# The heads' output-gate and bonus products of a hybrid decoder block formed from float32r parts with exact remainders

## The chip, the cores and the metric

The kernel runs on one core of one Trainium2 chip. The metric is the device time of one execution in microseconds (us), median of the runs. The five queues of the core are called by their engines: PE (TensorE: matrix products, with PEld for its weight loads), DVE (VectorE), ACT (ScalarE), POOL (GpSimd) and SP (SyncE, which issues nearly all DMA transfers). Each engine works its own queue in order and waits on semaphores for the others.

## The reference, cut to what matters

One decoder block over 256 tokens, width 2048, everything in float32: an RWKV-7 branch of 16 heads of 64 and a sliding-window attention branch of 16 heads work beside each other, are gated, added and projected, and a squared-ReLU MLP of width 8192 follows. The change touches two products of the RWKV branch, the gate `g` (160 gate inputs by 1024 columns) and the bonus (a sum over each head's 64 channels):

```python
p = h @ w_in[l] + b_in[l]                     # r, k, v, wd, ad, gd are columns of it
g = jax.nn.sigmoid(gd) @ g2                   # gd: 256 x 160, g2: 160 x 1024
...
y = rwkv7_scan(r_h, hs(decay), k_h, v_h, -kk, kk * a_h)
yn = ((y - mu) * lax.rsqrt(var + RWKV_GN_EPS)).reshape(B, T, C)
yn = yn * ln_w.astype(jnp.float32) + ln_b.astype(jnp.float32)
bonus = jnp.sum(r_h * k_h * r_k.astype(jnp.float32), axis=-1, keepdims=True) * v_h
out = (yn + bonus.reshape(B, T, C)) * g.astype(jnp.float32)
```

## The kernel before, in words

Activations lie transposed: channels on the 128 partitions, 256 tokens along the free axis. **The weight products** make up most of the time. Their weights come in blocks of 512 KB (tile `raw`, DMA of L286 on SP; the adaLN matrix in tiles `ada`, L141, which take their buffers from the same ring of 7). `split` (L264) halves each block into two float32r parts: ACT casts it to `whi` (L274), and DVE subtracts to get the exact remainder `wlo` (L275). `feed` (L297) and `rows_product` (L319) then form hi·hi, hi·lo and lo·hi products on PE, one float32r instruction each. Products of plain float32 tiles, with no such parts, remain in the heads' own work; there each product is two records in the trace.

**The RWKV heads** go through in four pieces (ss = 0 to 3) of four heads, two blocks of 128 channels each; every piece computes, per block i: the decay and key terms, `km` (r·k·r_k, one buffer), the products of `ar` with `bn` and `ke` (L566), which are masked into `tt` and stored to DRAM (`scr`, L573), the bonus product of `km` with the block-diagonal ones `bones` (L576), whose result is multiplied by v (L577), and transposes by identity products (`turned64`, L478). Two pieces at a time share one inversion of 16x16 blocks (`inverse16`): a load of `scr` into a tile of tag `lg` (L611), 30 small operations on POOL, two stores (L622, L624) and eight loads (L629), all on SP's queue. The products of the levels (L644, L653, L683) use what those loads bring. The output (`output`) normalises y, scales it on ACT (L745), loads the block's columns of g2 into a tile `lg` of two buffers (L748 for 128 of its rows, L749 for 32), transposes y (L478) and forms the gate product against `sgd` (L754, 128 rows) and `sgd2` (L755, 32 rows) in the same PSUM tile; ACT's L757, DVE's L759 and L760 finish the block.

**Order.** The code is written as three queues of generator steps (adaLN, attention, RWKV) which `pulse` advances by fixed rates while the weight blocks go by; from that, and from the buffers, a scheduler with a cost estimate of its own makes one fixed list of instructions for each engine and for SP. A tile of a tag with one buffer can't be written until the last reader of the one before is done.

## Time and profile before

| | |
|---|---|
| median of 3 runs | 1566.24 us (1565.78 to 1566.56) |
| the profiled execution | 1566.93 us, of which its span is 1565.1 us |
| PE busy | 1510.9 us, 97% of the span |
| DVE busy | 1100.7 us, 70% |
| ACT busy | 722.6 us, 46% |
| mean granted PE clock | 0.987 of full speed |
| moved by DMA | 372.80 MB, 238 GB/s in the mean |

The heads' work lies between about 190 and 700 us, the MLP behind 780 us. A start time in the rows below is us from the beginning of the span. A timeline row groups like neighbours: its second number lasts from the first one's start to the last one's end, and since products overlap in their pipeline, what a group costs is read from its start to the start of the next group.

### The profile page before, as it was taken

What the parts mean: (1) busy time and instruction counts of PE and PEld (TensorE: products, weight loads), DVE (VectorE), ACT (ScalarE), POOL (GpSimd) and SP (SyncE); (2) the same over time, 40 slices, a digit from 0 to 9 for tenths busy, and PEclk for the clock granted to TensorE, in tenths of its full rate; (3) what the DMA queues carried; (4) which work ended last, traced back from release to release, by engine and by line L of the source; (5) the groups of instructions that cost most, each with busy time, mean ns of one, the idle gap of its engine ahead of it and who ended that gap; (6) DMA issues with size and microseconds to landing.
All of it is one profiled execution on the core that took longest, in us unless ns stands there. A gap on an engine that the chain in (4) does not pass through costs nothing.

```text
span 1565.1 us, 30120 instructions
## 1 busy us (share of the span) xinstructions
PE 1510.9 (97%) x12122; PEld 1385.8 (89%) x12122; DVE 1100.7 (70%) x1784; ACT 722.6 (46%) x1107; POOL 40.5 (3%) x97
## 2 busy tenths in 40 slices
...
GB/s 343 335 325 295 342 234 245 245 170 310 283 262 285 269 155 297 282 147 339 285 215 173 240 222 228 216 222 226 225 228 211 227 222 205 184 188 189 194 183 81
DMA packets 297100, 372.80 MB, mean 238 GB/s; under 512 B 40912, under 2 KB 198384, under 8 KB 296320
## 3 DMA queue, kind: packets, MB, share of 16 engines
...
q0 software_dynamic: 512, 0.15, 0.1%
q14 instruction: 45, 0.37, 0.1%
...
## 4 chain that ended last, share of the span: by engine, by line
PE 87%; DVE 4%; DMA 3%; ACT 2%; issue 2%; POOL 1%; SPq 0%; POOLq 0%; DVEq 0%; ACTq 0%
PE mm L297 41%; PE mm L319 14%; PE ax L319 14%; PE ax L297 9%; PE ax L683 2%; PE ax L186 1%; PE ax L478 1%; DVE wlo L275 1%; DVE acc L219 1%; PE ax L566 1%; DMA ada<-in_w_ada_dram 1%; ACT whi L274 1%; DMA tt<-in_x_dram 1%; PE ax L653 0%; PE ax L237 0%
## 5 line engine op out<-in xcount | busy, mean ns | idle before, releaser
L274 ACT CAST whi<-raw 128x1024 fp32r<-128x1024 f32 x458 | 478.0, 1047 | 673.4 <-PE mm L297 257.0
L275 DVE TENSOR_TENSOR wlo<-raw,whi 128x1024 fp32r<-128x1024 f32 x458 | 557.0, 1219 | 267.3 <-ACT whi L274 258.6
L297 PE MATMUL mm<-h,whi 128*128 128x256 f32 (+1 forms) x3296 | 446.8, 286 | 3.4 <-ACT whi L274 3.4
L297 PEld LDWEIGHTS mm<-h,whi 128*128 128x128 f32 (+1 forms) x3296 | 415.2, 192 | 10.1 <-ACT whi L274 3.4
L219 DVE SCALAR_TENSOR_TENSOR acc<-ada,cact,acc 128x512 f32<-128x512 f32 x330 | 247.0, 749 | 60.2 <-DMA ada<-in_w_ada_dram 55.6
L297 PE MATMUL mm<-h,wlo 128*128 128x256 f32 (+1 forms) x1648 | 237.7, 284 | 0.0
L297 PEld LDWEIGHTS mm<-h,wlo 128*128 128x128 f32 (+1 forms) x1648 | 215.0, 191 | 1.1 <-issue 0.7
L319 PE MATMUL mm<-whi,u 128*128 128x512 f32 x512 | 138.3, 392 | 0.0
L319 PE MATMUL ax<-whi,u 128*128 128x512 f32 x512 | 138.0, 391 | 0.0
L297 PE MATMUL ax<-h,whi 128*128 128x256 f32 x768 | 109.0, 290 | 9.0 <-DVE p L969 4.5
L319 PEld LDWEIGHTS ax<-whi,u 128*128 128x128 f32 x512 | 96.2, 188 | 21.0
L319 PEld LDWEIGHTS mm<-whi,u 128*128 128x128 f32 x512 | 95.6, 188 | 20.2
L297 PEld LDWEIGHTS ax<-h,whi 128*128 128x128 f32 x768 | 100.2, 197 | 11.4 <-ACT whi L274 5.0
L319 PE MATMUL ax<-wlo,u 128*128 128x512 f32 x256 | 79.4, 391 | 0.0
L319 PE MATMUL mm<-wlo,u 128*128 128x512 f32 x256 | 79.3, 391 | 0.0
L297 PE MATMUL ax<-h,wlo 128*128 128x256 f32 x384 | 59.2, 287 | 0.0
L319 PEld LDWEIGHTS mm<-wlo,u 128*128 128x128 f32 x256 | 48.1, 188 | 10.5
L319 PEld LDWEIGHTS ax<-wlo,u 128*128 128x128 f32 x256 | 48.1, 188 | 10.5
L297 PEld LDWEIGHTS ax<-h,wlo 128*128 128x128 f32 x384 | 52.6, 197 | 0.1
L297 PE MATMUL mm<-tt,whi 128*128 128x256 f32 x256 | 37.7, 298 | 2.1 <-ACT tt L768 2.1
L297 PEld LDWEIGHTS mm<-tt,whi 128*128 128x128 f32 x256 | 34.5, 203 | 3.2 <-ACT tt L768 2.3
L319 PE MATMUL mm<-whi,m 128*128 128x512 f32 x128 | 35.0, 392 | 0.0
...
## 6 DMA issues: line engine op xcount, KB each, us to landing
ada<-in_w_ada_dram SPq DMA_DIRECT2D x192, 512.0 KB, 5.5
raw<-in_w_up_dram SPq DMA_DIRECT2D x128, 512.0 KB, 3.9
raw<-in_w_down_dram SPq DMA_DIRECT2D x128, 512.0 KB, 4.0
raw<-in_w_in_dram SPq DMA_DIRECT2D x72, 512.0 KB, 5.2
raw<-in_w_in_dram SPq DMA_DIRECT2D x128, 256.0 KB, 5.1
raw<-in_w_out_dram SPq DMA_DIRECT2D x32, 512.0 KB, 6.1
raw<-in_w_branch_attn_dram SPq DMA_DIRECT2D x16, 512.0 KB, 5.9
raw<-in_w_branch_rwkv_dram SPq DMA_DIRECT2D x16, 512.0 KB, 5.2
```

The costliest lines, as they stand in the source:

```text
L186: TE.matmul(ps[:, j:j + 1], lhsT=acc[:, j * P:(j + 1) * P], rhs=ones[:, 0:1], start=True, stop=True)
L219: V.scalar_tensor_tensor(o, in0=t[:, a, :], scalar=ck, in1=o, op0=ALU.mult, op1=ALU.add)
L274: S.copy(hi[:], raw[:])
L275: V.tensor_tensor(lo[:], raw[:], hi[:].bitcast(F32), op=ALU.subtract)
L297: TE.matmul(ps[0:m, j * tw:(j + 1) * tw], lhsT=wt[:, kk, o:o + m], rhs=xx(k), start=(k == begin and xx is xh and wt is hi and j == 0), sto ...
L319: TE.matmul(pss[tb][:], lhsT=uu(k)[:, sl], rhs=wt[:, kk, :], start=(first and k == 0), stop=(final and k == kblocks - 1))
L478: TE.matmul(out[hs, :], lhsT=src[hs, chunk(c)], rhs=ident[hs, hs], start=True, stop=True)
L566: TE.matmul(pT[hs, o:o + P], lhsT=src[hs, chunk(c)], rhs=ar[hs, i, c].rearrange("p a b -> p (a b)"), start=True, stop=True)
L683: TE.matmul(ps[hs, j, i, part, :], lhsT=lhs(j, i, hs), rhs=rhs(j, i, hs), start=(first and j == 0 and i == 0), stop=True, skip_group_check ...
```

## The change

Both kinds of product are formed from float32r parts, the way the weight products are. A helper `parts(hi, lo, x_)` casts on ACT and subtracts on DVE.

- **Bonus:** `km` is split into two tiles of tag `yn` (two buffers), and `bones` is cast once to `bonr`. One float32 product becomes two float32r ones (L584 and L585 in the changed kernel). `km` is free when DVE's subtraction has read it, no longer when PE has.
- **Gate:** `sgd` and `sgd2` are split once into `sgh`, `sgl` and the pair `sg2`; each block's g2 columns are split into `lh` and `ll` (one buffer each) from `lg`, which now has one buffer instead of two. Two float32 products a block become three of 128 rows (L767) and three of 32 rows (L769). `inverse16` takes the same single `lg` buffer.

```diff
--- before.py
+++ after.py
@@ -441,9 +441,10 @@
     tw = mx.tile([P, T], F32, name="tw")
-    sgd = mx.tile([P, T], F32, name="sgd")
-    kd = mx.tile([P, 2, T], F32, name="kd")
-    sgd2 = kd[0:32, 0, :]
+    sgh, sgl = [mx.tile([P, T], F32R, name=n) for n in ("sgh", "sgl")]
+    bonr = mx.tile([P, P], F32R, name="bonr")
+    kd = tl("kd", (2, T))
+    sg2 = []
     HS = [slice(0, L), slice(L, 2 * L)]
     state = [mx.tile([P, 2, 2, L], F32, name=nm("state")) for _ in range(2)]
@@ -471,6 +472,11 @@
+
+    def parts(hi, lo, x_):
+
+        S.copy(hi, x_)
+        V.tensor_tensor(lo, x_, hi.bitcast(F32), op=ALU.subtract)
     def turned64(out, src, c):
@@ -573,7 +579,10 @@
                 nc.sync.dma_start(square(scr[u:u + 4]).rearrange("u s t -> s u t"), tt[HS[p], 4 * i:4 * i + 4, 0, 0:L])
             yield
             pbn = ps_ax()
-            TE.matmul(pbn[:, 0:T], lhsT=bones, rhs=km[:], start=True, stop=True)
+            kmh, kml = [tl("yn", (T,), 2, F32R) for _ in range(2)]
+            parts(kmh[:], kml[:], km[:])
+            TE.matmul(pbn[:, 0:T], lhsT=bonr[:], rhs=kmh[:], start=True, stop=False)
+            TE.matmul(pbn[:, 0:T], lhsT=bonr[:], rhs=kml[:], start=False, stop=True)
             V.tensor_tensor(bv[:, i, :], vT, pbn[:, 0:T], op=ALU.mult)
             for n, (src, dst) in enumerate(((bn[:], "bt"), (ke, "kt"), (vT, "vt"))):
                 if n == 1:
@@ -607,7 +616,7 @@
     def inverse16(dds):
-        a16 = tl("lg", (16, 16), 2)
+        a16 = tl("lg", (16, 16))
         nc.sync.dma_start(a16[:], blocks16(scr[:]))
         x16 = tl("p4", (2, 16, 16), 2)
         tmp = tl("rs", (L,), 2)
@@ -743,16 +752,21 @@
             for c in range(NCH):
                 yc = y[:, i, chunk(c)]
                 S.activation(yc, yc, AF.Identity, bias=rd[:, 4 + c:5 + c], scale=rd[:, c:c + 1])
-            lg = tl("lg", (2, P), 2)
+            lg = tl("lg", (2, P))
             cl = slice(b * P, (b + 1) * P)
             nc.sync.dma_start(lg[:, 0, :], rwkv_g2[0:P, cl])
             nc.sync.dma_start(lg[0:32, 1, :], rwkv_g2[P:P + 32, cl])
             yield
+            lh, ll = [tl(n, (2, P), 1, F32R) for n in ("lh", "ll")]
+            for ks in ((slice(0, P), 0), (slice(0, 32), 1)):
+                parts(lh[ks], ll[ks], lg[ks])
             pF = ps_ax()
             for c in range(NCH):
                 turned64(pF[:, c * L:(c + 1) * L], y[:, i, :], c)
-            TE.matmul(pF[:, T:], lhsT=lg[:, 0, :], rhs=sgd[:], start=True, stop=False)
-            TE.matmul(pF[:, T:], lhsT=lg[0:32, 1, :], rhs=sgd2, start=False, stop=True)
+            for q, (w_, x_) in enumerate(((lh, sgh), (lh, sgl), (ll, sgh))):
+                TE.matmul(pF[:, T:], lhsT=w_[:, 0, :], rhs=x_[:], start=(q == 0), stop=False)
+            for q, (w_, x_) in enumerate(((lh, sg2[0]), (lh, sg2[1]), (ll, sg2[0]))):
+                TE.matmul(pF[:, T:], lhsT=w_[0:32, 1, :], rhs=x_, start=False, stop=(q == 2))
             yo = tl("yn", (T,), 2)
             S.activation(yo[:], pF[:, 0:T], AF.Identity, bias=colB[:, B_LB + b:B_LB + b + 1],
                          scale=colB[:, B_LW + b:B_LW + b + 1])
@@ -878,9 +892,12 @@
     def begin_heads():
         shifted(tw, e_l[:, 0:T], P, 24)
         S.activation(tw[0:L, :], tw[0:L, :], AF.Tanh)
+        sgd = tl("yn", (T,), 2)
         shifted(sgd, e_l[:, T:2 * T], P, 25)
         S.activation(sgd[:], sgd[:], AF.Tanh, scale=0.5)
         V.tensor_scalar(sgd[:], sgd[:], 1.0, 0.5, op0=ALU.add, op1=ALU.mult)
+        parts(sgh[:], sgl[:], sgd[:])
+        S.copy(bonr[:], bones)
         in0, in1 = [tl("in", (3, 2, T), 2) for _ in range(2)]
         for n, ((_, a_b), e) in enumerate(zip(A_RKV, (e_k, e_r, e_v))):
             for i in range(2):
@@ -995,9 +1012,13 @@
     def gd2():
         ps = cols_product(w_in, KC, O_WD + 256, [32], hA, hB)
+        sgd2 = tl("yn", (T,), 2)[0:32, :]
         shifted(sgd2, ps[0:32, 0:T], 32, 26)
         S.activation(sgd2, sgd2, AF.Tanh, scale=0.5)
         V.tensor_scalar(sgd2, sgd2, 1.0, 0.5, op0=ALU.add, op1=ALU.mult)
+        t = tl("kd", (2, T), 1, F32R)
+        sg2.extend(t[0:32, i, :] for i in range(2))
+        parts(*sg2, sgd2)
     def keyed(ss):
         for n in range(3):
```

Counted over PE's whole list, 24 float32 products of 128x256 go and 64 float32r products come; the stretches of float32r products between float32 ones number 123 before and 137 after.

Three places in the lists of instructions. First PE, at the first two heads' bonus products of the first two pieces (270 to 282 us before); L566 is L572 in the changed kernel, L478 is L484. Before:

```order
L297 MATMUL mm_2967<-h_219,wlo_3082 128x256 x8
L576 MATMUL ax_3113<-km_2934,kt 128x256
L478 MATMUL ax_3125<-kt,p_358_2633 64x64 x8
L297 MATMUL mm_2967<-h_219,whi_3177 128x256
L297 MATMUL mm_2967<-h_221,whi_3177 128x256
L478 MATMUL ax_3113<-kt,cs_2938 64x64 x8
L478 MATMUL ax_3125<-kt,in_2490 64x64 x8
```

and before, the second block's products, a little further on:

```order
L566 MATMUL ax_3022<-ar_2645,p_367_2650 64x128 x2
L566 MATMUL ax_3022<-ar_2645,cs_2952 64x128 x2
L566 MATMUL ax_3022<-ar_2645,p_367_2650 64x128 x2
L566 MATMUL ax_3032<-ar_2645,p_367_2650 64x128 x2
L566 MATMUL ax_3032<-ar_2645,cs_2952 64x128 x2
L566 MATMUL ax_3032<-ar_2645,p_367_2650 64x128 x2
L576 MATMUL ax_3144<-km_2948,kt 128x256
L478 MATMUL ax_3156<-kt,p_367_2650 64x64 x8
```

After:

```order
L297 MATMUL mm_2973<-h_219,wlo_3088 128x256 x2
L572 MATMUL ax_3028<-ar_2651,p_369_2656 64x128 x2
L572 MATMUL ax_3028<-ar_2651,cs_2958 64x128 x2
L572 MATMUL ax_3028<-ar_2651,p_369_2656 64x128 x2
L572 MATMUL ax_3038<-ar_2651,p_369_2656 64x128 x2
L572 MATMUL ax_3038<-ar_2651,cs_2958 64x128 x2
L572 MATMUL ax_3038<-ar_2651,p_369_2656 64x128 x2
L297 MATMUL mm_2973<-h_219,wlo_3088 128x256 x6
L584 MATMUL ax_3119<-yn_3120,bonr 128x256
L585 MATMUL ax_3119<-yn_3121,bonr 128x256
L484 MATMUL ax_3136<-kt,p_360_2639 64x64 x8
L584 MATMUL ax_3155<-yn_3156,bonr 128x256
```

What moved: the second block's six L572 rows now stand ahead of both bonus products, and its L584 stands close behind the first block's.

Second, SP around the first inversion (317 to 347 us before), with the semaphores each waits for; L611, L622, L624 and L748 are L620, L631, L633 and L757 in the changed kernel. The numbers in the names count tiles: raw_4150, 4191, 4249 and 4319 before are raw_4176, 4217, 4275 and 4345 after; ada_4187, 4279 and 4349 are ada_4213, 4305 and 4375. Before:

```order
L573 DMA scr<-tt_3021 64x4x64 [waits DMAHW1_49]
L286 DMA raw_4191<-in_w_in_dram 128x4x256 [waits DMAHW2_49,DVE_49]
L939 DMA grd<-gr_3814 128x512 [waits DMAHW3_49,Activation_49]
L611 DMA lg_3955<-scr 128x16x16 [waits DMAHW4_49,DMAHW1_49,DMAHW0_49]
L286 DMA raw_4249<-in_w_in_dram 128x4x256 [waits DMAHW5_49,DVE_49]
L141 DMA ada_4279<-in_w_ada_dram 128x2x512 [waits DMAHW6_49,DVE_49]
L748 DMA lg_5492<-in_rwkv_g_dram 128x128 [waits DMAHW7_49]
L286 DMA raw_4319<-in_w_in_dram 128x4x256 [waits DVE_49]
L141 DMA ada_4349<-in_w_ada_dram 128x2x512 [waits DVE_49]
L622 DMA scr_245<-p_536_3957 128x16x16 [waits DMAHW2_49,Pool_49]
```

After:

```order
L286 DMA raw_4176<-in_w_in_dram 128x4x256 [waits DMAHW0_49,DVE_49]
L620 DMA lg_3981<-scr 128x16x16 [waits DMAHW5_49,DMAHW6_49,DMAHW2_49,DMAHW1_49]
L141 DMA ada_4213<-in_w_ada_dram 128x2x512 [waits DVE_49]
L956 DMA grd<-gr_3840 128x512 [waits DMAHW3_49,Activation_49]
L286 DMA raw_4217<-in_w_in_dram 128x4x256 [waits DMAHW4_49,DVE_49]
L286 DMA raw_4275<-in_w_in_dram 128x4x256 [waits DVE_49]
L757 DMA lg_5522<-in_rwkv_g_dram 128x128 [waits DMAHW1_49,Pool_49]
L631 DMA scr_247<-p_546_3983 128x16x16 [waits DMAHW7_49,Pool_49]
L633 DMA scr_247<-p_546_3983 128x16x16 [waits DMAHW0_49,Pool_49]
L141 DMA ada_4305<-in_w_ada_dram 128x2x512 [waits DVE_49]
```

What moved: the g2 load (L757) waits for POOL; raw_4345 and ada_4375 left the place ahead of the two stores, and ada_4305 now stands behind them. On DVE the same weight blocks, before:

```order
L843 TENSOR_TENSOR m_3805<-m_3805 128x4
L844 RECIPROCAL m_3805<-m_3805 128x4
L219 SCALAR_TENSOR_TENSOR acc_4186<-ada_4349,cact,acc_4186 128x512
L275 TENSOR_TENSOR wlo_4119<-raw_4116,whi_4118 128x1024
L219 SCALAR_TENSOR_TENSOR acc_4186<-ada_4349,cact,acc_4186 128x512
L275 TENSOR_TENSOR wlo_4153<-raw_4150,whi_4152 128x1024
```

After:

```order
L857 TENSOR_TENSOR m_3831<-m_3831 128x4
L858 RECIPROCAL m_3831<-m_3831 128x4
L275 TENSOR_TENSOR wlo_4145<-raw_4142,whi_4144 128x1024
L219 SCALAR_TENSOR_TENSOR acc_4212<-ada_4305,cact,acc_4212 128x512 x2
L275 TENSOR_TENSOR wlo_4179<-raw_4176,whi_4178 128x1024
L275 TENSOR_TENSOR wlo_4220<-raw_4217,whi_4219 128x1024
```

What moved: ahead of the remainder of the block raw_4176 (`wlo_4179`) DVE now works on `ada_4305`, a tile that SP issues behind the inversion's stores; before, ahead of the same block's remainder (`wlo_4153`), it worked on `ada_4349`, issued ahead of them.

Third, PE at the gate products of the last two blocks (688 to 694 us before). Before:

```order
L478 MATMUL ax_8575<-kt,p_1004_7834 64x64 x2
L754 MATMUL ax_8575<-sgd,lg_8541 128x256
L755 MATMUL ax_8575<-kd,lg_8541 128x256
L478 MATMUL ax_8592<-kt,p_1004_7834 64x64 x8
L754 MATMUL ax_8592<-sgd,lg_8572 128x256
L755 MATMUL ax_8592<-kd,lg_8572 128x256
L186 MATMUL ax_8794<-kt,acc_7882 128x1 x4
L297 MATMUL mm_8845<-tt_8405,wlo_8849 128x256 x8
```

After:

```order
L484 MATMUL ax_8718<-kt,p_1032_7924 64x64 x2
L297 MATMUL mm_8975<-tt_8495,wlo_8979 128x256
L484 MATMUL ax_8718<-kt,p_1032_7924 64x64 x2
L769 MATMUL ax_8691<-kd_5438,lh_8685 128x256 x2
L769 MATMUL ax_8691<-kd_5438,ll_8686 128x256
L297 MATMUL mm_8975<-tt_8495,whi_9008 128x256
L297 MATMUL mm_8975<-tt_8496,whi_9008 128x256
L297 MATMUL mm_8975<-tt_8495,whi_9008 128x256
L297 MATMUL mm_8975<-tt_8496,whi_9008 128x256
L767 MATMUL ax_8718<-sgh,lh_8712 128x256
L767 MATMUL ax_8718<-sgl,lh_8712 128x256
L767 MATMUL ax_8718<-sgh,ll_8713 128x256
```

What moved: a block's L767 and L769 products stand apart, with other rows between them, and the last block's L767 (`lh_8712`) comes behind the L769 of the block before it, which reads `lh_8685` from the same single buffer.

## Rows read from the trace of the kernel before

**Rows 1.** The page: busy time of each engine.

```profile
PE 1510.9 (97%) x12122; PEld 1385.8 (89%) x12122; DVE 1100.7 (70%) x1784; ACT 722.6 (46%) x1107; POOL 40.5 (3%) x97
```

**Rows 2.** PE busy by stretch: span, PE (count), PEclk, DMA share, GB/s.

```profile
341.40:345.00 3.60, 3.54 (x33) 1.00 0.02 5
541.00:544.40 3.40, 3.40 (x18) 0.50 1.05 368
900.00:1100.00 200.00, 200.00 (x1319) 1.00 0.72 223
```

**Rows 3.** PE's timeline, 270 to 274 us: start, us, engine, line, operation, out<-in, shape, count.

```profile
270.47 1.12 PE L297 MATMUL mm<-h,wlo 128*128 128x256 f32 x8
271.43 0.59 PE L576 MATMUL ax<-km,kt 128*128 128x256 f32 x2
271.95 0.68 PE L478 MATMUL ax<-kt,p 64*64 64x64 f32 x16
272.56 0.50 PE L297 MATMUL mm<-h,whi 128*128 128x256 f32 x2
273.00 0.68 PE L478 MATMUL ax<-kt,cs 64*64 64x64 f32 x16
273.51 0.63 PE L478 MATMUL ax<-kt,in 64*64 64x64 f32 x16
```

**Rows 4.** PE's timeline, 456 to 458 us, first block's gate products.

```profile
456.01 0.70 PE L754 MATMUL ax<-sgd,lg 128*128 128x256 f32 x2
456.64 0.69 PE L755 MATMUL ax<-kd,lg 32*128 32x256 f32 x2
457.27 0.68 PE L478 MATMUL ax<-kt,p 64*64 64x64 f32 x16
```

**Rows 5.** Lines L768, L769, split of a 128x256 tile: count, ns min/median/max, first, last.

```profile
L768 ACT CAST tt<-yn x4: 392/397/404, 684.1 to 695.8; 128x256 fp32r<-128x256 f32 x4
...
L769 DVE TENSOR_TENSOR tt<-yn,tt x4: 418/419/420, 685.1 to 697.5; 128x256 fp32r<-128x256 f32 x4
```

**Rows 6.** SP's timeline, 326 to 348 us (DMA issues).

```profile
326.00 0.97 SPq L611 DMA_DIRECT2D lg<-scr  x1
346.02 0.37 SPq L622 DMA_DIRECT2D scr<-p  x1
347.45 1.13 SPq L286 DMA_DIRECT2D raw<-in_w_in_dram  x1
```

**Rows 7.** ACT's timeline, 352 us: a cast that waited for its DMA.

```profile
352.27 1.05 ACT L274 CAST whi<-raw 128x1024 fp32r<-128x1024 f32 x1 [2.17 <-DMA raw<-in_w_in_dram]
```

**Rows 8.** The page's DMA issues (count, KB each, us to landing): the adaLN tiles.

```profile
ada<-in_w_ada_dram SPq DMA_DIRECT2D x192, 512.0 KB, 5.5
```

**Rows 9.** The page's groups (count, busy, mean ns, idle before): adaLN sums on DVE.

```profile
L219 DVE SCALAR_TENSOR_TENSOR acc<-ada,cact,acc 128x512 f32<-128x512 f32 x330 | 247.0, 749 | 60.2 <-DMA ada<-in_w_ada_dram 55.6
```

**Rows 10.** DVE's timeline, 340 us: remainders of two weight blocks.

```profile
340.05 2.46 DVE L275 TENSOR_TENSOR wlo<-raw,whi 128x1024 fp32r<-128x1024 f32 x2
```

**Rows 11.** PE's timeline, 314 to 352 us; in brackets the idle time before.

```profile
314.75 0.68 PE L576 MATMUL ax<-km,kt 128*128 128x256 f32 x2
319.76 0.70 PE L576 MATMUL ax<-km,kt 128*128 128x256 f32 x2
341.39 0.43 PE L862 MATMUL ax<-a,vtok 128*64 128x128 f32 x2 [2.10 <-ACT a L857]
351.73 1.12 PE L297 MATMUL mm<-h,wlo 128*128 128x256 f32 x8
```

**Rows 12.** PE's timeline, 540 us.

```profile
539.79 0.71 PE L537 MATMUL ax<-kt,yn 128*128 128x128 f32 x4 [1.81 <-ACT yn L521]
```

**Rows 13.** PE's timeline, 690 to 694 us, the last two blocks' gate products.

```profile
690.39 0.70 PE L754 MATMUL ax<-sgd,lg 128*128 128x256 f32 x2
692.26 0.70 PE L754 MATMUL ax<-sgd,lg 128*128 128x256 f32 x2
693.51 1.05 PE L186 MATMUL ax<-kt,acc 128*128 128x1 f32 x8
```

**Rows 14.** Line L748, loads of 64 KB of g2: us from issue to landing.

```profile
DMA to landing us min/median/max: 1.9/3.4/7.3
```

## The prediction

> **What bounds the kernel now.** I read the page's busy times first, then busy time by stretch, then PE's timeline around the products that change, and last the queues that feed them. PE is busy for 97% of the span, DVE for 70%, ACT for 46% [rows 1]. In the MLP, 900 to 1100 us, PE has not a moment free [rows 2]; nothing is changed there. In the heads' part PE stops only in single places of up to about 2 us, such as 2.10 us in front of L862 and 1.81 us in front of L537 [rows 11, 12]. So a product that PE no longer has to form shortens the run by its own cost, unless the place behind it waits for something that didn't move, and a wait that the change adds on another queue costs time as soon as PE gets there first.
>
> **What PE saves.** A timeline row is priced from its start to the next start. The bonus product takes 0.52 us (271.43 to 271.95, behind float32r work) [rows 3]; a gate product takes 0.63, for 128 rows as for 32 (456.01, 456.64, 457.27) [rows 4]. A float32r product of the same 128x256 shape takes 0.12: eight from 270.47 to 271.43 [rows 3]. There are 8 bonus products and 16 gate products (two for each of 8 blocks).
> - Bonus: 8 x 0.58 (between 0.52 and 0.63, since they stand in both surroundings) less 16 x 0.12: 4.6 - 1.9 = 2.7 us.
> - Gate: 16 x 0.63 less 48 x 0.12: 10.1 - 5.8 = 4.3 us.
>
> Together 7.0 us. That isn't all: a switch between the two kinds costs. Two float32r products between two float32 groups take 0.44 us (272.56 to 273.00) where 2 x 0.12 is 0.24, so 0.20 is lost. Counted over PE's whole list, the runs of float32r products rise from 123 to 137, by 14. That takes 14 x 0.19 = 2.7 us back, which leaves **4.3 us**. For the bounds: at 0.3 a switch, the dearest that I read from the same rows if both edges count, 2.8 us are left. On the other side, sixteen transposes directly behind float32r work take 0.51 (273.00 to 273.51) and 0.61 behind a float32 product (271.95 to 272.56), so a switch also gives 0.10 back: then 14 x 0.1 = 1.4 is lost and 5.6 is saved.
>
> A rule of the Trainium skill speaks against a saving of that size. In these rows one float32 product costs 4.3 to 5.2 times a float32r one (0.52 and 0.63 by 0.12) [rows 3, 4]. The page "FP8 and Floating Point Precision", section "TensorE Precision Notes", says that a true fp32 product takes four passes through the array. By an exact four, an estimate from that page, a product would cost 0.48, the 24 would save 11.5 - 7.7 = 3.8 us, and after the switches 1.1 instead of 4.3. The measured rows decide here, and the sum stands on them.
>
> **What the splits cost.** A split of a 128x256 tile takes 0.40 us on ACT and 0.42 on DVE [rows 5]. There are 8 of `km`, two smaller ones for each of 8 blocks of g2, two for `sgd` and `sgd2`, and a cast of `bones`; priced all at full size, some 27 x 0.4 = 11 us on each of the two engines, in truth less, spread over more than 450 us. They lie beside PE's work. What hides them is the lead of the weight blocks: a remainder made from 340.05 on [rows 10] is first used at 351.73 [rows 11]; 0.4 us ahead of it change nothing. If that lead is gone, each costs its 0.4 on PE. I take nothing for them, except where the next two parts say so.
>
> **The first inversion.** Today 5.0 us lie between the two bonus products of the second piece (314.75 to 319.76) [rows 11], the second block's L566 products among them. In the new list these (L572) stand five float32r products behind the first bonus product, so their masks, the stores of `scr` and the load of L620 come some 2.5 to 3.5 us earlier. That load is issued at 326.00 now, and the store that needs POOL's result, L622, at 346.02, 20 us later; the next weight transfer goes out at 347.45 [rows 6]. Meanwhile SP's queue stands still. So the new store L631 is due about 343, and `ada_4305`, which now stands behind it and L633, about 1 us later, 343.7 to 344.9. The weight block issued at 347.45 let its cast begin at 352.27, 4.8 us later [rows 6, 7]; the adaLN tiles take 5.5 in the median [rows 8]. It lands between 348.5 and 350.4. On DVE it comes ahead of the remainder `wlo_4179`: two sums of 0.75 [rows 9] and 1.23 (half of 2.46) [rows 10], so the remainder is ready between 351.2 and 353.1. PE needs it where it now needs `wlo_4153`, at 351.73 [rows 11], less the about 1.1 us that four cheaper bonus products have brought by then: 350.6. The lead of ten us is gone, and PE **waits 0.6 to 2.5 us; I take 1.2**, near the lower end because the one measured landing in this very place is the short one. Queued behind it on DVE are the remainders of the blocks that follow and the sums that empty the gate products' PSUM tiles; they have several us more. The two weight tiles fewer ahead of the inversion cost nothing further: raw_4345 goes out behind the eight loads, but those also start some 3 us earlier.
>
> **The last gate products.** With one buffer of `lg`, `lh` and `ll` each, the last block's load of g2 (L757) can't go out before DVE has split the 32 rows of the block before, and these stand on ACT behind the eight scalings of y, which end at about the time that this block's gate product now starts, 690.39 [rows 13]. Cast and remainder of the smaller tile, about 0.3 each (less than the 0.40 and 0.42 of rows 5), make it about 691.0. Loads of this line land after 1.9 to 7.3 us, 3.4 in the median [rows 14]: 694.4, and with the cast 694.7. PE's order has ahead of the last L767 what stood behind it before, eight small products (0.92 us at 693.51 before) and some float32r ones, so it comes there about 693.5 instead of at 692.26 [rows 13]. The wait is **1.2 us** in the median, none with a fast load, 3 or more with a slow one. The other blocks' loads have the products of a whole block or more as cover; at the first blocks, where the lead is under 2 us, I take nothing.
>
> **The sum.** -4.3 + 1.2 + 1.2 = -1.9 us: 1565.0 against the profiled execution's 1566.93, of which the span is 1565.1 and 1.8 lie around it. The median of the runs, 1566.24, is 0.7 below that execution, so I take the difference from the median: **1564.3 us**.
>
> **Rivals.**
> - The whole gain arrives (chance 0.28). The inversion's result comes 4 us earlier, the load takes the 2 us that the fastest took, and neither wait is there: -4.3, or -5.6 with the cheap switch: 1561.9 (1560.6 to 1562.8). For it: all the waits rest on leads that I know to about 1 us. Against it: two queues must both come out well.
> - The clock takes the gain (0.16). After the 1.81 us of idle time at 539.79 the granted clock was 0.50 from 541.0 to 544.4 [rows 2, 12], the 1.2 GHz level instead of 2.4; half of 3.4 us is lost, 1.7. After the 2.10 us at 341.39 it stayed at 1.00 [rows 2, 11]. A new wait of over 1 us may go either way; one or both would make -0.2 to +1.5: 1566.0 to 1567.7, about 1566.4.
> - Slower (0.14): SP stands still too long in the first inversion. If POOL's result is no earlier than today, because its load of `scr` still waits for the queue ahead of it, `ada_4305` goes out at 347.5 and lands at 352.3 to 353, the remainder is ready at 355.5, and PE, there at 350.6, waits 5 us at half a clock's further cost, 1.7. That makes -4.3 + 5 + 1.7 + 1.2 = +3.6: about 1569.9. It decides from a landing of the adaLN tile behind 353; what speaks against it is the new place of the L572 products in PE's list.
> - The products don't become as cheap as they should (0.04): 0.2 instead of 0.12 for 64 small products with a weight load each would take 5.1 us, and the sum is +3.2: 1569.4. Against it: every float32r product of rows 3 has its own weight load too.
>
> **How the numbers follow.** Forecast 0.38 (1562.9 to 1565.7), the rivals 0.28, 0.16, 0.14 and 0.04. About 0.2%, 3.1 us, is what a measurement of this kernel can tell from no change, so faster begins under 1563.1 and slower over 1569.4. Faster: nearly all of the first rival and a small part of the forecast, 0.32. Slower: the third rival and half of the last, 0.16. The rest, 0.52, is the same within 0.2%. The range leaves out the best part of the first rival and the slower ones: 1561.2 to 1569.2.
>
> **What would show it.** The new rows L584, L585, L767 and L769 should cost 0.12 each from start to start, with 0.2 at a change of kind; the heads' part (190 to 700 us) should hold all of the difference, and the MLP none. PE should show a new idle row near 350 us ahead of an L297 of `wlo`, released by DVE, with DVE idle on an adaLN tile before it, and one near 693 us ahead of L767, released by ACT's `lh`. If neither is there, the first rival holds; if the clock by stretch is at 0.50 behind them, the second. The forecast is wrong from the ground if PE's busy time doesn't fall by some 3 to 5 us, or if the waits in front of L644, L862 or L537, which I leave as they are, change by more than 1 us.

## The result, and the profile after

| | before | after |
|---|---|---|
| median | 1566.4 us (12 runs, 1561.99 to 1568.34) | 1573.99 us (12 runs, 1565.88 to 1583.47) |
| profiled execution | 1566.93 us | 1573.24 us |
| PE busy | 1510.9 us | 1517.5 us |

The changed kernel is slower: the ratio is 1.0061, 95% interval 1.0039 to 1.0084 (this is the quotient of the means; that of the medians is 1.0048). The forecast was 1564.3 us in a range that ended at 1569.2; 1573.99 lies 4.8 us above that end.

The page's line of busy times, which answers to [rows 1], holds the first surprise: PE should have fallen by 3 to 5 us and rose by 6.6.

```profile
PE 1517.5 (97%) x12138; PEld 1394.3 (89%) x12138; DVE 1104.6 (70%) x1810; ACT 730.5 (46%) x1134; POOL 37.9 (2%) x97
```

A busy PE isn't a PE at full clock. PE by stretch in the changed kernel (as [rows 2]: span, PE, PEclk, DMA share, GB/s):

```profile
341.40:345.00 3.60, 3.60 (x33) 1.00 0.88 148
361.00:367.80 6.80, 4.10 (x66) 0.57 1.07 370
541.00:544.40 3.40, 3.02 (x25) 1.00 1.02 365
695.60:705.80 10.20, 10.00 (x44) 0.54 0.19 59
900.00:1100.00 200.00, 200.00 (x1319) 1.00 0.72 223
```

The MLP is as before. The stretch at 541 us, at half clock (1.2 GHz instead of 2.4) before, is at full clock now. Two new ones begin at 362 and at 696.4 us. The same two rows of the kernel before:

```profile
361.00:367.80 6.80, 6.80 (x105) 1.00 1.04 368
695.60:705.80 10.20, 10.20 (x78) 0.88 0.36 103
```

All stretches at half clock behind the first 60 us add up to 23.8 us before and 34.0 after; each costs half its length.

**Where the time went in this execution.** I took the float32r products of L297 and L319 from the 1000th to the 4300th, that is the heads' part (181.3 to 786.7 us before, 182.6 to 793.0 after), and put each interval down to one of three things: the work that PE does in it at full clock, idle time, or the excess at half clock.

| us | length | work at full clock | idle | lost to half clock |
|---|---|---|---|---|
| before | 605.4 | 581.7 | 15.9 | 7.8 |
| before, second profile | 603.5 | 581.8 | 15.6 | 6.1 |
| after | 610.4 | 581.0 | 16.7 | 12.7 |
| after, second profile | 614.7 | 581.5 | 20.2 | 13.1 |

The work fell by 0.7 and 0.3 us where 4.3 was forecast, idle time rose by 0.8 and 4.6, and half clock took 5 to 7 more. The runs say the same. Each run lists its span and mean granted clock, and span times (1 - clock) is what half clock took from it (the start of the kernel included, and idle time within such stretches). In the mean, before is 1565.6 us = 1547.5 + 18.1 of that loss (the 20 runs beside the first experiments), and after is 1575.4 = 1548.8 + 26.6 (12 runs): of 9.8 us, 8.5 are clock and 1.3 everything else. The standard errors of the two losses are 0.6 and 1.3 us. The spread of the runs is the clock's too: 1565.88 came at 0.987, 1583.47 at 0.979.

**The idle time** of PE, 180 to 790 us of the changed kernel (line, waited for: us, times, longest):

```profile
PE ax L653 <- DVE a L836: 4.0, 1, 4.0
PE ax L876 <- ACT a L871: 3.1, 3, 1.3
PE mm L297 <- ACT tt L782: 2.9, 1, 2.9
PE mm L297 <- DVE wlo L275: 2.9, 1, 2.9
...
PE ax L543 <- ACT yn L527: 0.4, 1, 0.4
```

The first row is new. Two waits of before are smaller: the 4.1 us that PE waited at the second inversion for the loads of the levels (L644) has become the 2.9 for `wlo`, and the 1.81 of [rows 12] is 0.4. So about 2.6 us came back there.

**The chain behind the 4.0 us** is to be read over four queues. SP's timeline, 339 to 355 us (in before, [rows 6]):

```profile
339.96 0.37 SPq L631 DMA_DIRECT2D scr<-p  x1
340.43 1.07 SPq L633 DMA_DIRECT2D scr<-p  x1
341.55 1.20 SPq L141 DMA_DIRECT2D ada<-in_w_ada_dram  x1
343.71 3.94 SPq L638 DMA_DIRECT2D in<-scr  x5
347.69 0.62 SPq L882 DMA_DIRECT2D yad<-a  x1
348.35 0.58 SPq L638 DMA_DIRECT2D in<-scr  x1
352.60 0.34 SPq L882 DMA_DIRECT2D yad<-a  x1
352.98 1.26 SPq L638 DMA_DIRECT2D in<-scr  x2
354.33 0.57 SPq L962 DMA_DIRECT2D rkvd<-gr  x1
354.94 0.43 SPq L286 DMA_DIRECT2D raw<-in_w_in_dram  x1
```

DVE's, ACT's and PE's timelines (one fence each, the same stretch; in brackets the idle time before and what ended it):

```profile
347.26 1.54 DVE L219 SCALAR_TENSOR_TENSOR acc<-ada,cact,acc 128x512 f32<-128x512 f32 x2 [9.81 <-DMA ada<-in_w_ada_dram]
348.72 2.36 DVE L275 TENSOR_TENSOR wlo<-raw,whi 128x1024 fp32r<-128x1024 f32 x2
350.99 0.48 DVE L439 SCALAR_TENSOR_TENSOR gr<-mm,colA,gr 128x255 f32<-128x255 f32 x1
...
361.95 1.22 DVE L275 TENSOR_TENSOR wlo<-raw,whi 128x1024 fp32r<-128x1024 f32 x1 [7.11 <-ACT whi L274]
363.10 1.01 DVE L836 SCALAR_TENSOR_TENSOR a<-kt,ax 128x384 f32<-128x384 f32 x2
```

```profile
351.50 0.56 ACT L437 ACTIVATE gr<-mm,colA,omm 128x255 f32<-128x255 f32 x1 [8.94 <-DVE gr L439]
360.88 1.04 ACT L274 CAST whi<-raw 128x1024 fp32r<-128x1024 f32 x1 [7.36 <-DMA raw<-in_w_in_dram]
```

```profile
363.70 2.61 PE L653 MATMUL ax<-in,tt 64*64 64x64 f32 x44 [4.02 <-DVE a L836]
```

The adaLN tile, now behind the two stores, goes out at 341.55, and DVE stands 9.81 us for it. Behind it on DVE are two remainders and then `gr` (L439), for which ACT stands 8.94 us. Behind that on ACT is what the second store to `yad` (L882) needs; SP stands for it from 348.93 to 352.60. Behind that on SP is the weight block `raw_4345`, issued at 354.94, whose cast starts at 360.88 and whose remainder ends at 363.2. In the kernel before the same block went out at 330.75, ahead of the stores, so its new place is a link of the chain too. Behind that on DVE stands L836, and L836 is what released PE's first products of the levels (L653, in the kernel before L644). One late tile goes round DVE, ACT, SP, a transfer, ACT and DVE again until PE feels it, 16 us after DVE began the tile's sum. Counted by products done, from the 1000th on, the changed kernel is 1.1 to 2.9 us ahead between 315 and 345 us and 3.4 behind at 366.

**The new products.** PE's timeline of a block's gate products, at full clock (as [rows 4]):

```profile
682.55 0.39 PE L767 MATMUL ax<-sgh,lh 128*128 128x256 f32 x1
682.77 0.28 PE L767 MATMUL ax<-sgl,lh 128*128 128x256 f32 x1
682.89 0.28 PE L767 MATMUL ax<-sgh,ll 128*128 128x256 f32 x1
683.11 0.50 PE L769 MATMUL ax<-kd,lh 32*128 32x256 f32 x2
683.44 0.27 PE L769 MATMUL ax<-kd,ll 32*128 32x256 f32 x1
683.65 0.45 PE L484 MATMUL ax<-kt,p 64*64 64x64 f32 x8
```

From start to start the six take 0.22, 0.12, 0.22, 0.33 for two, and 0.21: 1.10 us, where two float32 products took 1.26 [rows 4]. Only a product between two of its own kind and rows takes 0.12. The first behind the transposes, the last of 128 rows ahead of the 32-row ones, and the last of 32 rows ahead of the next transposes take 0.1 more. Over the heads' part, all 24 float32 products took 14.15 us (10.02 gate, 4.13 bonus) and the 64 new ones 12.47 (8.95 and 3.52), 0.195 each; the transposes beside them rose from 20.7 to 22.0.

**The tail.** The last block's load of g2 (SP), and its first and third product of 128 rows (PE; as [rows 13]):

```profile
695.82 0.33 SPq L757 DMA_DIRECT2D lg<-in_rwkv_g_dram  x1
```

```profile
698.49 0.54 PE L767 MATMUL ax<-sgh,lh 128*128 128x256 f32 x1
...
699.44 0.58 PE L767 MATMUL ax<-sgh,ll 128*128 128x256 f32 x1 [0.20 <-DVE ll L479]
```

The load goes out 4.8 us later than the 691 forecast, but PE, about 1 us late by then and at half clock from 696.4, waits only 0.2 for it. Between 672 and 705 us the changed kernel falls back by about another 4 us; 3.4 of these are the 10.2 us at half clock in place of 3.4.

### The profile page after: what moved, and what is told of

It is laid out like the page before. It is cut to its first block, busy times and chain, and to the rows that moved or that the text cites. A ratio compares the mean times of both kernels' runs of the same rounds, so it can differ in the third digit from the quotient of the medians.

```text
span 1571.5 us, 30208 instructions
## 1 busy us (share of the span) xinstructions
PE 1517.5 (97%) x12138; PEld 1394.3 (89%) x12138; DVE 1104.6 (70%) x1810; ACT 730.5 (46%) x1134; POOL 37.9 (2%) x97
## 4 chain that ended last, share of the span: by engine, by line
PE 83%; DVE 6%; DMA 4%; issue 2%; ACT 2%; POOL 2%; SPq 0%; POOLq 0%; DVEq 0%; ACTq 0%
PE mm L297 39%; PE mm L319 14%; PE ax L319 14%; PE ax L297 8%; DVE wlo L275 2%; PE ax L692 2%; DMA raw<-in_w_in_dram 1%; PE ax L186 1%; DVE acc L219 1%; DMA ada<-in_w_ada_dram 1%; PE ax L484 1%; POOL p L630 1%; PE ax L572 1%; POOL rs L628 1%; ACT whi L274 1%
## 5 line engine op out<-in xcount | busy, mean ns | idle before, releaser
L297 PE MATMUL mm<-h,whi 128*128 128x256 f32 (+1 forms) x3296 | 447.6, 286 | 3.4 <-ACT whi L274 3.4
L297 PEld LDWEIGHTS mm<-h,whi 128*128 128x128 f32 (+1 forms) x3296 | 415.4, 192 | 10.6 <-ACT whi L274 3.4
L297 PE MATMUL mm<-h,wlo 128*128 128x256 f32 (+1 forms) x1648 | 237.4, 284 | 2.9 <-DVE wlo L275 2.9
L297 PEld LDWEIGHTS mm<-h,wlo 128*128 128x128 f32 (+1 forms) x1648 | 214.8, 191 | 3.7 <-DVE wlo L275 3.1
L319 PE MATMUL mm<-whi,u 128*128 128x512 f32 x512 | 138.3, 392 | 0.0
L319 PE MATMUL ax<-whi,u 128*128 128x512 f32 x512 | 138.0, 391 | 0.0
L297 PE MATMUL ax<-h,whi 128*128 128x256 f32 x768 | 108.8, 290 | 8.9 <-DVE p L986 4.4
L319 PEld LDWEIGHTS ax<-whi,u 128*128 128x128 f32 x512 | 96.3, 188 | 21.0
L319 PEld LDWEIGHTS mm<-whi,u 128*128 128x128 f32 x512 | 95.7, 188 | 20.2
L297 PEld LDWEIGHTS ax<-h,whi 128*128 128x128 f32 x768 | 99.9, 196 | 11.3 <-ACT whi L274 5.0
L319 PE MATMUL ax<-wlo,u 128*128 128x512 f32 x256 | 79.4, 391 | 0.0
L319 PE MATMUL mm<-wlo,u 128*128 128x512 f32 x256 | 79.3, 391 | 0.0
L297 PE MATMUL ax<-h,wlo 128*128 128x256 f32 x384 | 59.6, 288 | 0.1
L319 PEld LDWEIGHTS ax<-wlo,u 128*128 128x128 f32 x256 | 48.1, 188 | 10.5
L319 PEld LDWEIGHTS mm<-wlo,u 128*128 128x128 f32 x256 | 48.1, 188 | 10.4
L297 PEld LDWEIGHTS ax<-h,wlo 128*128 128x128 f32 x384 | 53.0, 198 | 0.3 <-DVE wlo L275 0.3
L297 PE MATMUL mm<-tt,whi 128*128 128x256 f32 x256 | 40.0, 309 | 2.9 <-ACT tt L782 2.9
L297 PEld LDWEIGHTS mm<-tt,whi 128*128 128x128 f32 x256 | 36.5, 214 | 4.2 <-ACT tt L782 3.1
L319 PE MATMUL mm<-whi,m 128*128 128x512 f32 x128 | 35.3, 393 | 0.0
```

The lines of the kernel that those rows point to most:

```text
L297: TE.matmul(ps[0:m, j * tw:(j + 1) * tw], lhsT=wt[:, kk, o:o + m], rhs=xx(k), start=(k == begin and xx is xh and wt is hi and j == 0), sto ...
L319: TE.matmul(pss[tb][:], lhsT=uu(k)[:, sl], rhs=wt[:, kk, :], start=(first and k == 0), stop=(final and k == kblocks - 1))
```

## The experiments

The first four runs take the change apart; the next two are the best versions I found; two are second profiles; four try another queue; and the last four separate waits from products. In the table the loss to the clock and the rest are means over the runs, work and idle are the heads' part of the profile. The standard errors of the clock losses are 0.5 to 1.5 us. The kernel before, in the runs beside them, had medians of 1565.4 to 1566.4, a loss of 17.5 to 19.1 and a rest of 1547.1 to 1548.1.

| kernel | median | ratio, 95% | clock loss | rest | work | idle |
|---|---|---|---|---|---|---|
| after | 1573.99 | 1.0061 (1.0039 to 1.0084) | 26.6 | 1548.8 | 581.0 | 16.7 |
| bonus_only | 1574.42 | 1.0054 (1.0033 to 1.0076) | 25.3 | 1548.7 | 580.7 | 19.1 |
| gate_only | 1573.60 | 1.0065 (1.0040 to 1.0089) | 25.0 | 1550.1 | 583.1 | 20.7 |
| km_held | 1577.84 | 1.0094 (1.0068 to 1.0119) | 27.1 | 1551.4 | 584.8 | 17.5 |
| stack96 | 1571.07 | 1.0043 (1.0027 to 1.0058) | 23.5 | 1547.7 | 577.7 | 23.3 |
| gs_lg2 | 1567.68 | 1.0011 (0.9993 to 1.0030) | 21.4 | 1545.9 | 576.5 | 20.4 |
| bs_lg2 | 1567.25 | 1.0009 (0.9991 to 1.0027) | 21.7 | 1545.8 | 577.6 | 19.1 |
| before_pool4 | 1569.83 | 1.0029 (1.0014 to 1.0044) | 21.3 | 1549.2 | 581.5 | 19.3 |
| after_hihi | 1565.33 | 0.9999 (0.9985 to 1.0014) | 24.9 | 1540.8 | 573.6 | 18.2 |
| after_inv8 | 1564.81 | 0.9990 (0.9973 to 1.0008) | 22.8 | 1541.8 | 579.7 | 10.7 |
| before_inv8 | 1561.24 | 0.9965 (0.9951 to 0.9979) | 17.3 | 1543.8 | 580.4 | 13.2 |

### Each part alone

Bonus alone (the gate as before, `lg` with two buffers) and gate alone (the bonus as before):

```diff
 bonus_only
+            TE.matmul(pF[:, T:], lhsT=lg[:, 0, :], rhs=sgd[:], start=True, stop=False)
+            TE.matmul(pF[:, T:], lhsT=lg[0:32, 1, :], rhs=sgd2, start=False, stop=True)
 gate_only
+            TE.matmul(pbn[:, 0:T], lhsT=bones, rhs=km[:], start=True, stop=True)
```

> Only the bonus products are formed from parts; the gate products and the two buffers of lg stay as before. Theory: the wait of 4.0 us in front of L653 at the first inversion comes from the bonus part alone, because km is free as soon as DVE has read it and the order on SP and DVE changes with that. Then that wait (3 to 5 us, with a stretch at half clock behind it) is here too, the gate's tail (about 690 to 706 us) costs nothing, and the time is between 1565 and 1570 us. Rival: the single lg buffer, whose g2 load waits for POOL on SP's queue, makes the wait. Then there is no such wait here and the time is 1563 to 1564 us, the 2.7 us less that the cheaper products bring.

> Only the gate products are formed from parts, with lg, lh and ll in one buffer each; the bonus products stay float32. Theory: no wait of 4 us in front of the first inversion's level products, but the tail at 685 to 706 us costs about 4 us (late g2 loads, half clock), and the products themselves bring hardly anything: 1568 to 1571 us. Rival: the single lg buffer is what holds SP at the first inversion. Then the wait of 4 us is here and the time is 1573 to 1576 us.

Measured: 1574.42 and 1573.60. Both theories missed their times (up to 1570 and up to 1571). The gate's time is that of its rival, whose wait isn't there. Either half alone costs as much as both, so the costs don't add, and no account that sums a price of each product can explain the loss. Bonus alone has SP's order of the changed kernel at the first inversion, with the adaLN tile behind the stores, and its wait ahead of the levels, at less than half the length (PE's waits, 340 to 400 us; the other wait there, 3.2 us for ACT's copies of the attention, is in the kernel before too, with 3.0):

```profile
PE ax L653 <- DVE a L831: 1.8, 1, 1.8
```

This profile is of an execution of 1566.18 us, 8 us under the median of its kernel, and the heads' part lost 7.9 us to half clock in it, as before did (7.8); so it doesn't show where the slower runs lose theirs. Gate alone has the weight and adaLN tiles ahead of the stores as before and no such wait, but in its profile (an execution of 1582.61 us, 9 over the median) a wait at the first gate blocks, with half clock right behind it; PE's timeline, then PE by stretch:

```profile
458.48 0.37 PE L483 MATMUL ax<-kt,p 64*64 64x64 f32 x4 [2.12 <-ACT p L750]
```

```profile
459.20:469.40 10.20, 10.20 (x56) 0.53 0.62 206
```

### The early `km` undone

`km` is read once more behind the bonus product, so that its buffer comes free as late as before:

```diff
             TE.matmul(pbn[:, 0:T], lhsT=bonr[:], rhs=kml[:], start=False, stop=True)
+            held = tl("held", (4,))
+            V.tensor_tensor(held[:], km[:, 0:4], pbn[:, 0:4], op=ALU.mult)
```

> The whole change, but a tiny DVE operation that reads km and the bonus product's result keeps km's one buffer taken until PE has formed the product, as before the change. Nothing else is altered; eight operations of 4 columns are added. Theory: with km held, SP and DVE get back the order of before around the first inversion, the 4.0 us wait in front of the level products goes with its half-clock stretch, 5 to 6 us in all: 1567 to 1570 us. Rival: the early km has nothing to do with it, and the time stays at 1573 to 1575 us.

Measured: 1577.84, slower than the changed kernel. The inversion runs as late again as before (its load goes out at 324.41, its first store at 345.12), but SP's order isn't that of before: an adaLN tile still stands right behind the two stores, and goes out at 346.56. DVE stands even longer for it than in the changed kernel, and ACT 11.98 us for `gr` behind it (DVE's timeline):

```profile
351.71 0.75 DVE L219 SCALAR_TENSOR_TENSOR acc<-ada,cact,acc 128x512 f32<-128x512 f32 x1 [12.02 <-DMA ada<-in_w_ada_dram]
```

The wait ahead of the levels' first products is gone in this stretch, and another stands there that before lacks (PE's waits, 340 to 400 us):

```profile
PE ax L836 <- DVE gtc L188: 2.5, 1, 2.5
```

The forecast fell, and so did the rival's time. But since the edit left the late tile behind the stores, it isn't a test of the order on SP: it shows that holding `km` doesn't bring the order of before back. PE's work is 3.8 us above the changed kernel's as well; no run shows why.

### Fewer and like products

The three 32-row parts are stacked on 96 rows (three small loads instead of one), so that one product replaces three:

```diff
-            for q, (w_, x_) in enumerate(((lh, sg2[0]), (lh, sg2[1]), (ll, sg2[0]))):
-                TE.matmul(pF[:, T:], lhsT=w_[0:32, 1, :], rhs=x_, start=False, stop=(q == 2))
+            TE.matmul(pF[:, T:], lhsT=lh[0:96, 1, :], rhs=sg2[0], start=False, stop=True)
```

> The whole change, but the three 32-row gate products of a block are stacked into one product of 96 rows (hi, hi, lo of g2 against hi, lo, hi of the gate inputs), so that a block has four products instead of six. Theory: in the changed kernel six products cost 1.10 us, since a change between 128 and 32 rows costs about 0.1 us beside each product's 0.12, and up to 1.6 us where other products stand between them; four cost 0.7. Over eight blocks that is 2.5 to 4 us less on PE: 1570 to 1572 us. Rival: it is the late loads and buffers alone that cost in the tail, and the number of products doesn't matter: 1573 to 1575 us.

Measured: 1571.07, as expected, and the work fell by 3.3 us, as expected too. That the total came out is luck in part: idle time rose by 6.6 us in the profile, and of the 4.2 us that the mean fell 3.1 are clock. PE's timeline of one block:

```profile
685.31 0.38 PE L770 MATMUL ax<-sgh,lh 128*128 128x256 f32 x1
685.53 0.28 PE L770 MATMUL ax<-sgl,lh 128*128 128x256 f32 x1
685.65 0.28 PE L770 MATMUL ax<-sgh,ll 128*128 128x256 f32 x1
685.76 0.28 PE L771 MATMUL ax<-kd,lh 96*128 96x256 f32 x1
```

No time is lost between 128 and 96 rows here (0.12, 0.11). The 32 gate products take 4.72 us (3.31 and 1.41) instead of 8.95 for 48: the 16 that went took 0.26 each with the changes of rows.

Then the same with two buffers for `lg`, once with the bonus in float32 (gs_lg2) and once with everything (bs_lg2, where `ll` lies in a free half of `kd`):

```diff
-            lg = tl("lg", (2, P))
+            lg = tl("lg", (2, P), 2)
```

> Only the gate products are changed, the bonus products stay float32; the three 32-row products of a block are stacked into one of 96 rows, and lg keeps two buffers. SP's order around the first inversion is that of before, and no g2 load waits for POOL or for the split of the block before. Theory: what costs in the changed kernel is the late loads, the waits and the half-clock stretches behind them; without these the four products in place of two float32 ones leave 3 to 4 us less on PE: 1561 to 1564 us. Rival: any new arrangement of the heads' products brings 6 to 8 us more at half clock, whatever waits it has: 1568 to 1572 us.

> The same gate products with two buffers of lg, and the bonus products from parts as in the change; the second float32r half of a g2 block lies in the free half of another tile. SP and DVE have the changed kernel's order around the first inversion, with an adaLN tile issued behind the inversion's stores and worked on by DVE ahead of the weight remainders. Theory: the wait of 2 to 4 us in front of the first inversion's level products and the half clock behind it come back, as in the run with the bonus part alone, and eat what the gate products bring: 1566 to 1571 us. Rival: the bonus part costs nothing by itself: 1559 to 1563 us.

Measured: 1567.68 and 1567.25, no difference from before that these runs can tell. The work falls by 4 to 5 us, the gain that I had forecast for the change itself, and idle time (+3 to +4.5 in the profiles) and clock (+2.5 to +2.8 in the means) take it. The theory of gs_lg2 missed (it ended at 1564); bs_lg2 lies in its range, with a wait of 1.6 us ahead of L653 where 2 to 4 were forecast. No version that forms the whole output was faster than the kernel before.

### Second profiles

> The changed kernel once more, for a second profile. If the waits come from the order of the queues, the wait near 360 us in front of L653, released by DVE's L836, is here again at 2 us or more, with a stretch at half clock behind it, and the clock is low again for 6 us or more from about 695 us. If they were chance of one execution, they are elsewhere or gone.

> The kernel before once more, for a second profile. If its order is what keeps the clock up, there is again no half-clock stretch between 180 and 530 us and in all some 24 us of them (5 to 7 stretches of 3.4 us). If the first profile was a lucky one, there are stretches in the first inversion here too.

Measured: 1575.48 and 1566.99. The waits of the changed kernel repeat (4.1 us ahead of L653, 2.8 ahead of `wlo` at the second inversion), and so do 34.0 us at half clock; before has 20.4. One part of what I expected of before failed: its second profile has a stretch of 3.4 us at half clock in the first inversion too, from 345.1 us on, behind a wait of 2.7 us ahead of L862; in the first profile the wait there was 2.10 [rows 11], with no half clock behind it. So one profile of the changed kernel against one of before doesn't tell which stretch the change brings.

### POOL issues the inversion's transfers

So that SP needn't stand for POOL, POOL issues the two stores and eight loads itself, in four kernels (two lines stand for all; in the kernel before they are L622, L624 and L629):

```diff
-        nc.sync.dma_start(blocks16(scr2[0]), x16[:, 0])
+        nc.gpsimd.dma_start(blocks16(scr2[0]), x16[:, 0])
```

> The whole change, but the two stores and the eight loads of each inversion are issued by POOL instead of SP. SP then never stands behind the inversion's result; the adaLN tile that DVE works on ahead of the weight remainders goes out with the others. Theory: the chain SP, adaLN tile, DVE, ACT, SP makes the wait of 4.0 us in front of L653 and the half clock behind it (5 to 6 us of the loss). Then DVE's idle time of 9.8 us on that tile is gone or under 5 us, the wait near 360 us shrinks to under 2 us or is one for the loads themselves, and the time is 1567 to 1571 us. Rival: the level products wait for the inversion whatever the queue; then the wait stays at 3 us or more under another name, and the time at 1573 to 1577 us.

> The kernel before with nothing but the inversion's stores and loads issued by POOL: the control for the two runs beside it. Theory: before the change the queues' order has little to win at the first inversion, and the loads of the second one (4.1 us of waits) come neither earlier nor later by more than 1 us: 1563 to 1568 us, the same as before. Rival: SP's standing still costs in the kernel before as well: 1558 to 1562 us.

> Bonus from parts, gate with one stacked product of 96 rows in place of three of 32, two buffers of lg, and the inversion's stores and loads issued by POOL. Theory: without the wait at the first inversion (1.6 us and what stood behind it) the work saved on PE, about 4 us, becomes visible: 1560 to 1564 us. Rival: the loads come later from POOL than from SP and PE waits for them at both inversions: 1567 to 1572 us.

> Only the gate changed (one stacked product of 96 rows, two buffers of lg), bonus in float32, the inversion's stores and loads issued by POOL. Theory: as the kernel with the stacked gate alone, 3 to 4 us less work on PE, and less of the 2.9 us wait for the loads at the second inversion: 1562 to 1566 us. Rival: the clock is low as often as in that kernel and nothing is won: 1567 to 1570 us.

Measured: 1603.45, 1598.81, 1581.84 and 1588.53, ratios 1.0231, 1.0204, 1.0102 and 1.0148. The theory failed in all four. The loads of L638 (issue to landing) took in the changed kernel with POOL

```profile
DMA to landing us min/median/max: 2.9/5.3/8.5
```

against a median of 3.7 from SP, and POOL waits for its stores to land in between; at the second inversion PE waits 11 to 12 us for these loads in all four. The longer landing (4.7 to 6.4 us in the other three kernels, against 3.5 from SP in the kernel before) and POOL's waits for its stores (4.48 and 1.48 us at the second inversion of the changed kernel with POOL) are part of that; the rest isn't taken apart. At the first, DVE still waits for its adaLN tile, and PE behind it (DVE's, then PE's timeline):

```profile
343.36 0.75 DVE L219 SCALAR_TENSOR_TENSOR acc<-ada,cact,acc 128x512 f32<-128x512 f32 x1 [7.98 <-DMA ada<-in_w_ada_dram]
```

```profile
347.15 0.69 PE L876 MATMUL ax<-a,vtok 128*64 128x128 f32 x2 [8.52 <-ACT a L871]
```

That transfers issued from GpSimd take longer is what the Trainium skill says too, in "DMA: Bandwidth & Descriptors", section "Issuing engine by pattern": those of SP and ACT are generally faster. This run agrees (5.3 against 3.7 us).

### A wait of known size in the kernel before

Four copies more on POOL behind the last step of the first inversion. In the code they stand ahead of both stores, but the first store doesn't need what they write: they hold up the copy that the second store waits for. The lists of PE, DVE, ACT and SP stay instruction for instruction those of before:

```diff
+        if not getattr(tl, 'inv', 0):
+            tl.inv = 1
+            for _ in range(4):
+                G.tensor_copy(x16[:, 1], x16[:, 0].rearrange("p a b -> p b a"))
         nc.sync.dma_start(blocks16(scr2[0]), x16[:, 0])
```

> The kernel before, with four copies of 128x256 added to POOL's queue ahead of the first store of the first inversion; the lists of PE, DVE, ACT and SP are instruction for instruction those of before. A copy takes 0.63 us in the trace of before and the next starts 0.08 behind it, so SP's store and all that stands behind it go out 2.8 us later. Theory (a wait of some us in the heads' part costs itself and, behind it, stretches of half clock): PE gets an idle row of 1 to 3 us between 350 and 370 us, one more stretch at 0.50 behind it of 3.4 to 6.8 us, and the time is 1.5 to 5 us above the kernel before: 1567.5 to 1571, with PE's work in the heads' part as before (581.7 us). Rival (the half clock comes from small float32r products scattered among others, not from waits): no more stretches of half clock than before, and at most the wait itself, 0 to 2.8 us: 1566 to 1568.5.

Measured: 1569.83, 4.1 us over before (mean 4.8: 1.0 in the rest, 3.8 in the clock). The four copies took 3.6 us, not the 2.8 that I had reckoned; one of them took 1.5. The first store went out at 346.83, 0.8 later than before, and the second 4.5 later (346.71 before). POOL's, then SP's timeline:

```profile
346.87 3.60 POOL L625 COPY p<-p 128x256 f32<-128x256 f32 x4
```

```profile
351.19 0.37 SPq L628 DMA_DIRECT2D scr<-p  x1
```

PE's timeline, then PE by stretch:

```profile
379.04 0.52 PE L859 MATMUL ax<-kt,a 128*128 128x128 f32 x3 [2.43 <-ACT whi L274]
380.68 0.55 PE L859 MATMUL ax<-kt,a 128*128 128x128 f32 x3 [1.12 <-DVE in L658]
```

```profile
381.10:387.90 6.80, 5.69 (x35) 0.53 0.94 291
```

This is the cleanest of the runs: nothing but one queue's time is changed, and no product. PE feels it 30 us later, in two waits (before has 0.15 us there), with half clock on top, and in the means the clock's share is four fifths of the price (3.8 us, standard error 1.0). The profile by itself doesn't show that share: its heads' part lost 7.4 us to half clock, and the two profiles of before lost 7.8 and 6.1, because the stretches that the first of these has at 541 and 694 us are missing here. So that a delay alone costs clock is shown by the means over the runs; in which stretches, no run shows. The theory held; the rival (scattered small products as the cause) ended at 1568.5 and can't explain a loss without any change of products. My size of the idle time was right in sum (+3.4 us), from a delay that came out 0.8 us longer than I had reckoned, and its place was wrong (379 to 381 us instead of 350 to 370).

### Products taken away, waits left

Only hi times hi of each bonus and gate product:

```diff
-            for q, (w_, x_) in enumerate(((lh, sgh), (lh, sgl), (ll, sgh))):
+            for q, (w_, x_) in enumerate(((lh, sgh),)):
-            for q, (w_, x_) in enumerate(((lh, sg2[0]), (lh, sg2[1]), (ll, sg2[0]))):
+            for q, (w_, x_) in enumerate(((lh, sg2[0]),)):
-            TE.matmul(pbn[:, 0:T], lhsT=bonr[:], rhs=kml[:], start=False, stop=True)
```

> The changed kernel with only the hi times hi product of each bonus and gate product: 24 float32r products instead of 64, all splits and buffers as they are (the two remainder terms of each are left out of the output). Theory (the cost of the new products is in the switches and in the change of rows, not in the products): the 40 that go cost 0.12 each, 4.8 us of PE work at full clock, 576.2 us left of 581.0 in the heads' part; the wait of 4 us at the first inversion stays, so do the stretches of half clock: 1568 to 1570. Rival (each small product costs the 0.175 to 0.24 of its slot): 7 to 8 us of PE work go, 573.5 left. Second rival (the scattered small products themselves bring the half clock): there is less than half as much of it behind 650 us as in the changed kernel (10.2 us), and the time is 1563 to 1566.

Measured: 1565.33. The 40 products that went took 7.4 us of work with them (581.0 to 573.6), 0.185 each and not 0.12: the first rival's number, against my theory that they are cheap and only the switches cost. Half clock stays: 24.9 us in the mean, 26.6 with all products, and behind 650 us 10.2 us of it in the profile, 13.6 with all products. So the second rival fell: going from 64 small products to 24 doesn't take half clock away beyond the noise. PE's waits, 180 to 790 us:

```profile
PE ax L653 <- DMA in<-scr: 3.9, 3, 2.5
...
PE ax L653 <- DVE a L836: 3.0, 1, 3.0
```

The wait of the first inversion is there with 24 of the 64 products, and even a kernel that forms 24 float32r products in place of 24 float32 ones is no faster than before.

### Shorter inversions, products left

Both kernels with 8 of the 15 steps of both inversions:

```diff
-        for s in range(15):
+        for s in range(8):
```

> The changed kernel with 8 of the 15 steps of both inversions (the other 7, 14 operations of 0.21 to 0.65 us on POOL in the trace of before, are left out of the output); POOL's result comes about 4.5 to 5 us earlier, and SP stands that much shorter. Theory (the late adaLN tile behind SP's stores is what makes PE wait at the first inversion): DVE's wait of 9.8 us for the adaLN tile falls to 5 or less, PE's wait of 4.0 ahead of the second level goes to 0 to 1, the half clock behind it goes, and the time falls against the changed kernel by 4 to 8 us: 1566 to 1570. Rival (the wait only moves to the next place, as it did in the kernel without the early km): the sum of PE's idle time in the heads' part stays at 16 us or more, and the time at 1571 to 1575.

> Control: the kernel before with 8 of the 15 steps of both inversions, as in the run of the changed kernel with it. In the kernel before PE's waits at the first inversion are short, and 4.1 us of waiting for the second inversion's result could go. Theory: 0 to 4 us faster than before, 1562 to 1566, so that the changed kernel with short inversions comes to within 3 us of this one or below it. Rival (half clock and idle time move elsewhere): 1566 to 1568, and the distance between the two short-inversion kernels stays at 7 us or more.

Measured: 1564.81 and 1561.24. In the changed kernel all that is left of PE's waits between 340 and 400 us is this row, which the kernel before has too (3.0):

```profile
PE ax L876 <- ACT a L871: 2.8, 2, 1.9
```

The 4.0 and the 2.9 us at the two inversions are gone. The mean falls by 10.8 us in the changed kernel (7.0 in the rest, 3.8 in the clock) and by 4.5 in the one before (4.3 and 0.2). The distance between the two kernels shrinks from 9.8 to 3.5 us, and without the clock it turns: -2.0; in the profiles the changed one has 0.7 us less work and 2.5 less idle time. The standard error of the 3.8 us of clock is 1.8, and the profile, of an execution 1.9 us over the median, doesn't show it: its heads' part lost 13.5 us to half clock, the changed kernel's two profiles 12.7 and 13.1.

The changed kernel came out faster than the range of its theory: SP's stand from the inversion's load to its first store fell from 18.0 to 12.1 us, by more than the 4.5 to 5 reckoned, and three of the first inversion's operations left out had taken 1.2 us and more in the trace of before, not 0.65 at most. The distance of 3.5 just misses the 3 of the control's theory.

One reservation: the shorter inversion also changes SP's order in both kernels; in the changed one the adaLN tile now stands behind the eight loads and a weight block in its place, and in the short kernel before an adaLN tile now stands right behind the stores, without a wait ahead of the levels. So this run tells that most of the loss hangs on how long the inversions take, not which of the two cures it. What it leaves is 5.5 us of clock. In its profile the half clock that has no counterpart in the short kernel before lies at the gate's blocks, 10.2 us from 457.6 on behind a wait of 1.25 us, and 10.2 instead of 3.4 in the tail.

## Why the prediction was wrong, step by step

- **What PE saves: the term was mis-sized.** 4.3 us forecast, 0.3 to 0.7 measured. The float32 products were priced well (14.7 forecast, 14.15 measured). The 64 new ones cost 12.5 instead of 7.7 and 2.7 for switches, and the transposes beside them 1.3 more. I had read 0.12 from eight equal products in a row [rows 3] and counted only changes of kind; the new ones stand singly, and between 128 and 32 rows a change costs 0.1 too. The rival with 0.2 a product, which I gave 0.04, had the right price (0.195), though it still took 2.7 us for switches on top. The estimate by the four passes of the Trainium skill's page "FP8 and Floating Point Precision", section "TensorE Precision Notes", 1.1 us, came near the measured saving, but for another reason: the float32 products cost what rows 4 show, and it was the float32r ones that were dear.
- **The first inversion: right place, wrong chain.** SP's stand ended earlier than I said (L631 at 339.96, not about 343), the adaLN tile came in before 347.3 (forecast 348.5 to 350.4), and the wait that I expected, on the remainder `wlo_4179`, did not occur. The step that failed is the sentence that the two weight tiles cost nothing further because the eight loads start 3 us earlier. They do start earlier, but the stores of `yad` stand between them on SP, the second of these waits for ACT, ACT for DVE, and DVE for the late tile; `raw_4345` went out at 354.94 and PE waited 4.0 us for what stands behind its remainder. I had followed the tile to DVE's next reader and not to the queues that wait for DVE.
- **The tail: right row, wrong size.** The load was 5 us later than forecast and PE waited 0.2 instead of 1.2, since it came later as well; the loss of about 4 us there is half clock for the most part.
- **Waits left as they are: wrong, in the kernel's favour.** L644's 4.1 us became 2.9 and L537's 1.8 became 0.4, over the 1 us that I named as the limit.
- **The clock: the rival that was too small.** I gave it 0.16, one or two stretches and 1566.4 us. It is most of the loss, 8.5 of 9.8 us in the mean. That a delay brings it is shown by the means over the runs: 3.6 us more on POOL alone cost 3.8 us of clock (standard error 1.0) with the same lists elsewhere, and shorter inversions took 3.8 us (1.8) of it away. Single profiles show neither. That the number of the products brings it isn't borne out by after_hihi (24.9 us with 24 products, 26.6 with 64).
- **What stays open:** the last 5.5 us of clock loss, which remain when the inversion's waits are gone, and why each half of the change alone already costs as much as both. In the profiles of gate_only and after_inv8 such stretches begin behind waits of 1 to 2 us at the gate's blocks, and in the changed kernel's tail with hardly a wait; no run took them away singly. Nor did a run restore SP's order of before with all the new products in place: km_held was to do it and didn't.
